# Mixture-of-experts weights in chunks of two channel tiles by 1024 features, experts overlapped, w2 dealt four rows to a partition

## The chip, the cores and the metric

The kernel runs on one NeuronCore of one Trainium2 chip. The metric is the device time of one execution in microseconds, as the median of three runs. The five engines that matter are PE (matrix multiply), ACT (activation), DVE (vector), POOL, and SP, which here only issues DMAs. Each engine works off its own list of instructions in a fixed order and waits on semaphores for the others.

## The reference

Two layers of a hybrid model for 256 tokens of width 1024. Each layer has a mixer; layer 0 has a dense feed-forward part and layer 1 a mixture of eight experts with top-2 routing. The change touches the experts only:

```
logits = (h @ router)
top_v, top_i = lax.top_k(logits, TOP_K)
gates = jnp.sum(one_hot(top_i, N_EXPERTS) * softmax(top_v)[..., None], axis=-2)
for e in range(N_EXPERTS):
    out = out + gates[..., e:e + 1] * ((silu(h @ w1[e]) * (h @ w3[e])) @ w2[e])
```

Here h is 256 x 1024, w1 and w3 are 1024 x 3584 per expert, and w2 is 3584 x 1024, all in fp32. One expert has 44 MB of weights, all eight 352 MB.

## The kernel before

Weights come as chunks of 1 MB (128 partitions x 2048 fp32) that `load` (L128) fetches on the SP queue into a tile called raw. `stream` (L150) lists all chunks in the order of use, `place` (L190) says which buffer each goes to, and `take` (L215) hands the next one to the multiplication. Chunk i of the experts goes to a ring of ten buffers: four of tag raw, one more in pool mp, and five from the pool act, whose twelve 8 KB buffers of tag big also hold everything else that is large (the gathered inputs X, the scaled outputs yy, the sum acc, the token-major inputs tm).

Every matrix product is done in three fp32r passes (`mm3`, L228). For that each chunk is split, by halves of 1024 columns, into a rounded part and a rest (`split_act`, L221): ACT writes whi (L222), then DVE writes wlo = raw - whi (L223). There are four whi and four wlo buffers, so half k can only be split once PE has finished with half k - 4. One half feeds two mm3, which is six matmuls of 512 columns. `take` puts the splits of chunk i + 1 ahead of the matmuls of chunk i.

`moe` (L1076) routes up to 128 tokens to each expert. `slots` and `gather` (L1125) build X for two experts at a time by 32 small matmuls gx that ACT and DVE copy out (L1138, L1140). For each expert, seven groups j of 512 features follow. A group takes four chunks of w1 and w3 (each 4 channel tiles x 512 features, 2 KB of a row at a time) into two PSUM tiles h; ACT applies Silu (L1221), DVE multiplies (L1222) into u; four PE transposes ut (L1229) turn u round, and ACT and DVE split the result into us (L222, L223). `down(j)` then multiplies us by two chunks of w2 (4 KB of a row at a time) into the two PSUM tiles y. It is called for group j - 1 while group j is under way, and for group 6 at the end of the expert. After that `gated` (L1158) scales y by the gate into yy (ACT L1160, DVE L1161), and `scatter` (L1146) sends yy back to the tokens by 16 small matmuls so, in four pieces that DVE adds to acc (L1156) during the next expert. The pieces are hung between the chunks by `step()`. The gather for the next pair of experts stands inside `down(5)` and `down(6)` of every second expert. ut, so, gx and two smaller tiles share two PSUM buffers of pool pm, tag m.

The framework's scheduler turns these calls into the fixed order of each engine, and gives out the buffers; a tile that finds no buffer free is put later in the order.

```
hi, lo for a half of a chunk:
        a = self.nc.scalar.activation(hi, x, AF.Copy)
        b = self.nc.vector.tensor_tensor(lo, x, hi.bitcast(F), op=OP.subtract)
```

Of the kernel before, what the change touches and what calls it, by code (L numbers as in the profile page):

```python
# [9 lines left out]
F = mybir.dt.float32  # L10
# [84 lines left out]
class Kernel:  # L95
# [54 lines left out]
    def stream(self):  # L150
# [26 lines left out]
        v1, v3, v2 = (a["moe_w%d" % i][0].rearrange("e (k p) f -> e p k f", p=P) for i in (1, 3, 2))  # L177
        for e in range(NE):
            last = e == NE - 1
            for j in range(7):  # L180
                out += [v[e, :, 4 * h:4 * h + 4, j * 512:(j + 1) * 512] for v in (v1, v3) for h in range(2)]
                if j and not last:
                    out += [v2[e, :, 2 * c:2 * c + 2, :] for c in (2 * j - 2, 2 * j - 1)]
            if last:
                out += [v2[e, :, 4 * c:4 * c + 4, n * 512:(n + 1) * 512] for n in range(2) for c in range(NET // 4)]
            else:
                out += [v2[e, :, 2 * c:2 * c + 2, :] for c in (12, 13)]
        return out

    def place(self, i):  # L190
# [4 lines left out]
        ring = ("raw",) * 4 + ("more",) + ("big",) * 5  # L195
        if i >= (NE - 1) * 42:
            return ring[i % 5]
        if i < 10 + self.early:
            return ring[min(i, 9)]
        return ring[(i - self.early) % 10]  # L200
# [651 lines left out]
    def mixer(self, l, h):  # L852
# [70 lines left out]
        def mid(c):  # L923
            if c == 2 and l == DEPTH - 1:
                self.ahead(self.moe0 + self.early + 10, 0)
# [149 lines left out]
    def moe(self, h, r):  # L1075
# [95 lines left out]
        side = []  # L1171
        for e in range(NE):
            us = []
            if e == 0:
                side = [r.gates, None]
            else:
                side = [None, None] + [lambda p=p, e=e: scatter(e - 1, p) for p in range(4)]
            if e % 2 == 0:
                side += [lambda e=e: slots_t(e)]
            if e == 1:  # L1180
                side.append(count)
            side = iter(side)

            def step():
# [3 lines left out]
            last = e == NE - 1  # L1188
            py = [self.py.tile([P, 512], F, name=self.nm("y"), tag="y") for _ in range(2)]
            yy = self.big(R, "yy")  # L1190
            Y[e] = yy[:, :D], yy[:, D:]
            g = gather(e + 1) if e % 2 and not last else iter(())

            def down(j):

                for c in range(2):
                    W = self.take()
                    for k in range(2):
                        f = 2 * c + k
                        for n in range(2):  # L1200
                            self.mm3(py[n], [t[:, f] for t in us[j]], [x[:, n * 512:(n + 1) * 512] for x in W[k]],
                                     j == 0 and f == 0, j == 6 and f == 3)
                    if j > 4:
                        next(g, None)
                        next(g, None)
            for j in range(7):
                hs = []
                for v in range(2):
                    ps = self.pg.tile([P, 512], F, name=self.nm("h"), tag="g")
                    for a in range(2):  # L1210
                        W = self.take()
                        self.behind = None
                        for k in range(4):
                            self.mm3(ps, [x[:, 4 * a + k] for x in X[e]], W[k],
                                     a == 0 and k == 0, a == 1 and k == 3)
                        for _ in g0:
                            pass
                        step()
                    hs.append(ps)
                u = self.sm([P, 512], name="u")  # L1220
                nc.scalar.activation(u, hs[0], AF.Silu)  # L1221
                nc.vector.tensor_tensor(u, u, hs[1], op=OP.mult)  # L1222
                if j and not last:
                    down(j - 1)
                if j == 1 and e % 2 and not last:
                    slots(e + 1)
                pt = self.pm.tile([P, 4, P], F, name=self.nm("ut"), tag="m")
                for i in range(4):
                    nc.tensor.transpose(pt[:, i], u[:, i * P:(i + 1) * P], self.c("ident"))  # L1229
                if not last:  # L1230
                    t = self.mp.tile([P, 2, 4, P], R, name=self.nm("us"), tag="us", bufs=2)
                elif j % 2 == 0:
                    t2 = self.big(R, "us").rearrange("p (j a b t) -> p j a b t", j=2, a=2, b=4)
                if last:
                    t = t2[:, j % 2]
                self.split_act(pt, t[:, 0], t[:, 1])
# [249 lines left out]
```

## Time and profile before

| | |
|---|---|
| median of three runs | 1959.42 us (1958.44 to 1960.45) |
| the profiled execution | 1957.16 us |
| its span, first to last instruction | 1955.4 us |
| mean granted TensorE clock | 0.984 |
| busy share of the span: PE, DVE, ACT | 95%, 81%, 65% |
| DMA | 540.10 MB, q1 77.9% of the 16 engines' time |
| chain that ended last | PE 88%, DVE 4%, ACT 3%, DMA 2% |

Busy time is the time in which an engine executes at least one instruction; matmuls overlap, so the pace of PE is read from the distance between their starts. The experts begin at about 933 us and end at about 1942 us of the span.

### The profile page before, as it was taken

What the parts mean: (1) busy time and instruction counts of PE and PEld (TensorE: products, weight loads), DVE (VectorE), ACT (ScalarE), POOL (GpSimd) and SP (SyncE); (2) the same over time, 40 slices, a digit from 0 to 9 for tenths busy, and PEclk for the clock granted to TensorE, in tenths of its full rate; (3) what the DMA queues carried; (4) which work ended last, traced back from release to release, by engine and by line L of the source; (5) the groups of instructions that cost most, each with busy time, mean ns of one, the idle gap of its engine ahead of it and who ended that gap; (6) DMA issues with size and microseconds to landing.
All of it is one profiled execution on the core that took longest, in us unless ns stands there. A gap on an engine that the chain in (4) does not pass through costs nothing.

```text
span 1955.4 us, 32539 instructions
## 1 busy us (share of the span) xinstructions
PE 1867.3 (95%) x13258; PEld 1647.6 (84%) x13258; DVE 1583.8 (81%) x1839; ACT 1273.9 (65%) x1514; POOL 8.1 (0%) x11
## 2 busy tenths in 40 slices
PE   6999999899989989998999999999999999999996
PEld 3988999799979989997887887878878877787885
DVE  4678866777766788676899998999989898899996
ACT  4664744444446737444787787877878777787884
POOL 0000000000000000000000000000000000000000
PEclk8999999999999999999999999999999999999998
DMA  9544676477754437877799998999989999897994
GB/s 316 194 148 148 226 263 214 141 242 262 298 173 138 142 122 245 266 262 280 251 362 328 362 380 304 367 360 359 375 295 378 374 333 355 329 349 268 339 355 146
DMA packets 293790, 540.10 MB, mean 276 GB/s; under 512 B 8704, under 2 KB 132224, under 8 KB 293632
## 3 DMA queue, kind: packets, MB, share of 16 engines
q1 hardware_dynamic: 293632, 537.93, 77.9%
q8 instruction: 106, 1.74, 0.4%
q14 instruction: 52, 0.43, 0.1%
HBM read 536.85 MB, written 1.05 MB: 275 GB/s over the span
## 4 chain that ended last, share of the span: by engine, by line
PE 88%; DVE 4%; ACT 3%; DMA 2%; issue 1%; SPq 0%; ACTq 0%; DVEq 0%
PE h L231 10%; PE h L230 10%; PE h L232 10%; PE ps L230 10%; PE ps L231 10%; PE ps L232 10%; PE y L232 5%; PE y L230 5%; PE y L231 5%; DMA raw<-in_w_ada 1%; DVE wlo L223 1%; PE ut L1229 1%; PE po L230 1%; PE po L231 1%; PE po L232 1%
## 5 line engine op out<-in xcount | busy, mean ns | idle before, releaser
L222 ACT ACTIVATE whi<-raw 128x1024 fp32r<-128x1024 f32 x910 | 959.1, 1060 | 494.5 <-PE ps L231 203.9
L223 DVE TENSOR_TENSOR wlo<-raw,whi 128x1024 fp32r<-128x1024 f32 x910 | 1095.7, 1222 | 185.2 <-ACT whi L222 154.0
L230 PE MATMUL ps<-hhi,whi 128*128 128x256 f32 x1216 | 347.2, 286 | 11.1 <-ACT hhi L422 10.9
L230 PE MATMUL h<-whi,X 128*128 128x512 f32 x896 | 353.7, 395 | 0.0
L231 PE MATMUL h<-wlo,X 128*128 128x512 f32 x896 | 350.5, 391 | 0.4 <-DVE wlo L223 0.4
L232 PE MATMUL h<-whi,X 128*128 128x512 f32 x896 | 350.1, 391 | 0.0
L231 PE MATMUL ps<-hlo,whi 128*128 128x256 f32 x1216 | 346.2, 285 | 0.1
L232 PE MATMUL ps<-hhi,wlo 128*128 128x256 f32 x1216 | 345.4, 284 | 0.1
L230 PEld LDWEIGHTS ps<-hhi,whi 128*128 128x128 f32 x1216 | 234.4, 193 | 14.2 <-ACT hhi L422 11.7
L231 PEld LDWEIGHTS ps<-hlo,whi 128*128 128x128 f32 x1216 | 234.5, 193 | 2.0 <-issue 1.0
L232 PEld LDWEIGHTS ps<-hhi,wlo 128*128 128x128 f32 x1216 | 234.3, 193 | 1.3 <-issue 0.8
L231 PEld LDWEIGHTS h<-wlo,X 128*128 128x128 f32 x896 | 168.7, 188 | 35.7 <-DVE wlo L223 3.0
L232 PEld LDWEIGHTS h<-whi,X 128*128 128x128 f32 x896 | 168.4, 188 | 35.3
L230 PEld LDWEIGHTS h<-whi,X 128*128 128x128 f32 x896 | 168.7, 188 | 32.9
L230 PE MATMUL y<-whi,us 128*128 128x512 f32 (+1 forms) x452 | 174.1, 389 | 4.3 <-ACT us L222 4.3
L231 PE MATMUL y<-wlo,us 128*128 128x512 f32 (+1 forms) x452 | 175.7, 389 | 0.4 <-DVE wlo L223 0.4
L232 PE MATMUL y<-whi,us 128*128 128x512 f32 (+1 forms) x452 | 174.7, 389 | 0.5 <-DVE us L223 0.5
L285 DVE SCALAR_TENSOR_TENSOR ada<-raw,ca,ada 128x1024 f32<-128x1024 f32 x70 | 89.7, 1282 | 44.0 <-DMA raw<-in_w_ada 43.6
L230 PEld LDWEIGHTS y<-whi,us 128*128 128x128 f32 x452 | 84.9, 188 | 22.4 <-ACT us L222 5.2
L232 PEld LDWEIGHTS y<-whi,us 128*128 128x128 f32 x452 | 84.6, 188 | 19.1 <-DVE us L223 1.8
L231 PEld LDWEIGHTS y<-wlo,us 128*128 128x128 f32 x452 | 84.9, 188 | 18.1 <-DVE wlo L223 1.3
L230 PE MATMUL ps<-ghi,whi 128*128 128x256 f32 x256 | 72.5, 283 | 0.0
(349 smaller groups left out, 2303.4 us busy)
## 6 DMA issues: line engine op xcount, KB each, us to landing
raw<-in_moe_w SPq DMA_DIRECT2D x336, 1024.0 KB, 6.4
raw<-in_w_in SPq DMA_DIRECT2D x64, 1024.0 KB, 6.9
raw<-in_w_ada SPq DMA_DIRECT2D x48, 1024.0 KB, 7.6
raw<-in_ffn_w SPq DMA_DIRECT2D x33, 1024.0 KB, 5.6
raw<-in_w_proj_a SPq DMA_DIRECT2D x8, 1024.0 KB, 7.2
raw<-in_w_proj_b SPq DMA_DIRECT2D x8, 1024.0 KB, 7.8
raw<-in_w_out SPq DMA_DIRECT2D x8, 1024.0 KB, 5.3
wbd<-in_wbd SPq DMA_DIRECT2D x8, 512.0 KB, 8.4
```

The source lines that it names most:

```text
L222: a = self.nc.scalar.activation(hi, x, AF.Copy)
L223: b = self.nc.vector.tensor_tensor(lo, x, hi.bitcast(F), op=OP.subtract)
L230: first = nc.tensor.matmul(ps, l[0], r[0], start=start, stop=False, **k)
L231: nc.tensor.matmul(ps, l[0], r[1], start=False, stop=False, **k)
L232: nc.tensor.matmul(ps, l[1], r[0], start=False, stop=stop, **k)
L285: o = nc.vector.scalar_tensor_tensor(acc, w, self.ca[:, k:k + 1], acc, op0=OP.mult, op1=OP.add)
L1229: nc.tensor.transpose(pt[:, i], u[:, i * P:(i + 1) * P], self.c("ident"))
```

## The change

Chunks of w1 and w3 become 2 channel tiles x 1024 features (4 KB of a row at a time); the last 512 of the 3584 features keep the old shape. The rows of w2 are dealt so that a partition holds four that follow one another; a chunk takes two of them (8 KB in one piece), and the columns of u are picked at a distance of four for the transposes, to match. An expert now has four groups j, three of 1024 features (two PSUM tiles and two of every step after them) and one of 512. The last `down` of an expert and its `gated` move behind the first group of the next expert. The small steps are hung at fixed places: scatter at chunks 11, 13, 15 and 17 of w1 and w3, the next gather at chunks 12, 14, ... 26 of every second expert. us moves from two buffers of its own in pool mp to the pool act (tag big), the ring of weight buffers becomes 4 raw + 2 in mp + 2 big, and loads are asked for ten chunks ahead in place of twelve.

```diff
-            raw = self.mp.tile([P, 2048], F, name=self.nm("raw"), tag="raw", bufs=1)
+            raw = self.mp.tile([P, 2048], F, name=self.nm("raw"), tag="raw", bufs=2)
...
+        v2 = a["moe_w2"][0].rearrange("e (b p i) c -> e b p i c", p=P, i=4)
         for e in range(NE):
             last = e == NE - 1
-            for j in range(7):
-                out += [v[e, :, 4 * h:4 * h + 4, j * 512:(j + 1) * 512] for v in (v1, v3) for h in range(2)]
-                if j and not last:
-                    out += [v2[e, :, 2 * c:2 * c + 2, :] for c in (2 * j - 2, 2 * j - 1)]
+            for j in range(4):
+                if j < 3:
+                    out += [v[e, :, 2 * h:2 * h + 2, j * 1024:(j + 1) * 1024] for v in (v1, v3) for h in range(4)]
+                else:
+                    out += [v[e, :, 4 * h:4 * h + 4, 3072:] for v in (v1, v3) for h in range(2)]
+                if j == 0 and e:
+                    out += [v2[e - 1, 6, :, 2 * c:2 * c + 2, :] for c in range(2)]
+                elif j and not last:
+                    out += [v2[e, b, :, 2 * c:2 * c + 2, :] for b in (2 * j - 2, 2 * j - 1) for c in range(2)]
...
-        ring = ("raw",) * 4 + ("more",) + ("big",) * 5
+        ring = ("raw",) * 4 + ("more",) * 2 + ("big",) * 2
...
-        self.ahead(i + 4 if i < self.moe0 else i + 10 + self.early, i + (3 if i + 1 in self.pairs else 2))
+        self.ahead(i + 4 if i < self.moe0 else i + 10, i + (3 if i + 1 in self.pairs else 2))
...
+            side = {}
+            if e == 0:
+                side[0] = r.gates
+            else:
+                for p in range(4):
+                    side[11 + 2 * p] = lambda p=p, e=e: scatter(e - 1, p)
+            if e % 2 == 0:
+                side[19] = lambda e=e: slots_t(e)
+            elif not last:
+                side[9] = lambda e=e: slots(e + 1)
+                g = gather(e + 1)
+                for i in range(8):
+                    side[12 + 2 * i] = lambda: next(g)
...
+            for j in range(4):
+                n = 2 if j < 3 else 1
+                u = []
                 for v in range(2):
+                    ps = [self.pg.tile([P, 512], F, name=self.nm("h"), tag="g") for _ in range(n)]
+                    up(e, ps, v, j, side)
+                    for i in range(n):
+                        if v == 0:
+                            u.append(self.sm([P, 512], name="u"))
+                            nc.scalar.activation(u[i], ps[i], AF.Silu)
+                        else:
+                            nc.vector.tensor_tensor(u[i], u[i], ps[i], op=OP.mult)
+                if j == 0 and e:
+                    down(*before, 3)
+                    halves(e - 1)
+                    for i in range(2):
+                        gated(e - 1, slice(i * 512, (i + 1) * 512), before[1][i])
...
                 if j and not last:
+                    down(us, py, j - 1)
+                t = self.big(R, "us").rearrange("p (a b t) -> p a b t", a=2, b=8)
+                for i in range(n):
+                    pt = self.pm.tile([P, 4, P], F, name=self.nm("ut"), tag="m")
+                    for k in range(4):
+                        nc.tensor.transpose(pt[:, k], u[i].rearrange("p (t k) -> p k t", k=4)[:, k], self.c("ident"))
+                    o = slice(4 * i, 4 * i + 4)
+                    self.split_act(pt, t[:, 0, o], t[:, 1, o])
```

The changed file's lines stand 5 further down for `split_act` and `mm3` (L227, L228, L235 to L237).

First place: DVE, before the change, in a middle group of the third expert. A product u is followed by five splits of weights and then by us of the same group; PE uses that us 48 h matmuls later.

```order
L1222 TENSOR_TENSOR u_12994<-u_12994,h_12949 128x512
L223 TENSOR_TENSOR wlo_13004<-raw_12735,whi_13003 128x1024
L223 TENSOR_TENSOR wlo_13022<-raw_12763,whi_13021 128x1024
L223 TENSOR_TENSOR wlo_13026<-raw_12763,whi_13025 128x1024
L223 TENSOR_TENSOR wlo_13053<-raw_12792,whi_13052 128x1024
L223 TENSOR_TENSOR wlo_13057<-raw_12792,whi_13056 128x1024
L223 TENSOR_TENSOR us_13046<-ut_13041,us_13046 128x512
```

DVE after the change, third expert, at the end of the short group (3072 to 3583). us_13411 belongs to the group before; its transposes came 48 h matmuls earlier.

```order
L228 TENSOR_TENSOR wlo_13503<-raw_13299,whi_13502 128x1024
L1238 TENSOR_TENSOR u_13471<-u_13471,h_13473 128x512
L228 TENSOR_TENSOR wlo_13522<-raw_13323,whi_13521 128x1024
L228 TENSOR_TENSOR wlo_13526<-raw_13323,whi_13525 128x1024
L228 TENSOR_TENSOR us_13411<-ut_13412,us_13411 128x512
L228 TENSOR_TENSOR us_13411<-ut_13419,us_13411 128x512
```

PE after the change at the same place: the last h matmuls of the short group, and right behind them the y matmuls that read us_13411.

```order
L235 MATMUL h_13473<-whi_13480,X_11826 128x512
L236 MATMUL h_13473<-wlo_13481,X_11826 128x512
L237 MATMUL h_13473<-whi_13480,X_11827 128x512
L235 MATMUL y_13013<-whi_13498,us_13411 128x512
L236 MATMUL y_13013<-wlo_13499,us_13411 128x512
L235 MATMUL y_13014<-whi_13498,us_13411 128x512
L237 MATMUL y_13013<-whi_13498,us_13411 128x512
```

The split of us has moved from long before its use to behind a product that itself waits for the last h matmul.

Second place: DVE after the change, fifth expert, end of the first group. The two products u of a group stand apart, with the two splits of one chunk between them.

```order
L228 TENSOR_TENSOR wlo_14860<-raw_14661,whi_14859 128x1024
L1238 TENSOR_TENSOR u_14803<-u_14803,h_14807 128x512
L228 TENSOR_TENSOR wlo_14878<-raw_14683,whi_14877 128x1024
L228 TENSOR_TENSOR wlo_14882<-raw_14683,whi_14881 128x1024
L1238 TENSOR_TENSOR u_14805<-u_14805,h_14808 128x512
```

PE after the change at that place: wlo_14878 is read by the matmuls behind the transposes.

```order
L237 MATMUL h_14808<-whi_14859,X_13995 128x512
L235 MATMUL y_14088<-whi_14877,us_14705 128x512
L235 MATMUL y_14089<-whi_14877,us_14705 128x512
L1252 MATMUL ut_14949<-cst,u_14803 128x128 x4
L236 MATMUL y_14088<-wlo_14878,us_14705 128x512
```

The first split of the down chunk now stands behind a product that waits for PE, where before the change a split of the next chunk had been done by then.

Third place: DVE after the change, third expert, end of its first group, where the scaling of the second expert's outputs has moved to.

```order
L228 TENSOR_TENSOR wlo_12914<-raw_12699,whi_12913 128x1024
L1166 SCALAR_TENSOR_TENSOR yy_12789<-y_11920,gs_10395,yy_12789 128x512
L1166 SCALAR_TENSOR_TENSOR yy_12789<-y_11921,gs_10395,yy_12789 128x512
L228 TENSOR_TENSOR us_12794<-ut_12795,us_12794 128x512
L228 TENSOR_TENSOR us_12794<-ut_12802,us_12794 128x512
L228 TENSOR_TENSOR wlo_12918<-raw_12699,whi_12917 128x1024
L1161 TENSOR_TENSOR acc_10396<-acc_10396,so_12899 128x512
```

Four steps that are no weight splits now stand in one row on DVE; before the change the scaling and us stood apart.

## Rows read from the trace of the kernel before

**Rows 1.** Busy time by stretch (us from the span's start), the experts and one undisturbed stretch

```profile
core 0: us, PE busy (x) PEld busy (x) DVE busy (x) ACT busy (x) POOL busy (x), PEclk, DMA share, GB/s
950.00:1930.00 980.00, 964.71 (x4440) 793.61 (x4439) 895.70 (x848) 766.37 (x806) 0.00 (x0) 1.00 0.94 343
1200.00:1300.00 100.00, 100.00 (x462) 82.86 (x461) 94.12 (x91) 79.89 (x83) 0.00 (x0) 1.00 0.98 359
```

**Rows 2.** DMA queue of SP in the experts' stretch: longest waits, issues

```profile
SPq L135 <- DVE wlo L223: 814.3, 264, 15.3
...
raw<-in_moe_w SPq DMA_DIRECT2D x321, 1024.0 KB, 6.4
```

**Rows 3.** PE in order of time, an undisturbed stretch: start, duration, instruction

```profile
1073.98 0.40 PE L232 MATMUL h<-whi,X 128*128 128x512 f32 x1
1074.21 0.60 PE L1229 MATMUL ut<-cst,u 128*128 128x128 f32 x4
1074.57 0.48 PE L230 MATMUL h<-whi,X 128*128 128x512 f32 x1
```

**Rows 4.** PE in order of time, end of the first expert; in brackets idle time, releaser

```profile
1052.45 0.60 PE L1229 MATMUL ut<-cst,u 128*128 128x128 f32 x4
1054.25 0.50 PE L230 MATMUL y<-whi,us 128*128 128x512 f32 x1 [1.19 <-ACT us L222]
...
1055.05 0.40 PE L231 MATMUL y<-wlo,us 128*128 128x512 f32 x1
1055.62 0.74 PE L232 MATMUL y<-whi,us 128*128 128x512 f32 x2 [0.17 <-DVE us L223]
```

**Rows 5.** The same, end of the second expert

```profile
1174.77 0.39 PE L232 MATMUL y<-whi,us 128*128 128x512 f32 x1
1176.79 0.74 PE L1135 MATMUL gx<-Pm,tm 128*128 128x256 f32 x4 [1.63 <-ACT X L1140]
1178.25 0.71 PE L1135 MATMUL gx<-Pm,tm 128*128 128x256 f32 x4 [0.73 <-DVE X L1138]
...
1179.75 0.74 PE L1135 MATMUL gx<-Pm,tm 128*128 128x256 f32 x4 [0.35 <-DVE X L1138]
```

**Rows 6.** The same, first scatter of the sixth expert

```profile
1581.90 0.39 PE L1152 MATMUL so<-PT,yy 128*128 128x256 f32 x1 [1.00 <-DVE yy L1161]
...
1583.31 0.66 PE L1229 MATMUL ut<-cst,u 128*128 128x128 f32 x4 [0.42 <-DVE acc L1156]
```

**Rows 7.** Waits from 950 to 1930 us: who for whom, us in total, times, longest

```profile
PE gx L1135 <- ACT X L1140: 4.9, 3, 1.6
PE y L230 <- ACT us L222: 4.3, 4, 1.2
...
PE gx L1135 <- DVE X L1138: 3.4, 6, 0.9
```

**Rows 8.** Instruction groups from 950 to 1930 us: count, busy us, mean ns, idle before

```profile
L223 DVE TENSOR_TENSOR wlo<-raw,whi 128x1024 fp32r<-128x1024 f32 x663 | 797.7, 1222 | 72.1 <-ACT whi L222 41.8
L222 ACT ACTIVATE whi<-raw 128x1024 fp32r<-128x1024 f32 x662 | 697.9, 1061 | 181.9 <-PE h L232 110.5 <-PE y L232 59.3 <-DVE wlo L223 10.8
...
L223 DVE TENSOR_TENSOR us<-ut,us 128x512 fp32r<-128x512 f32 x56 | 38.3, 685 | 6.0 <-ACT us L222 6.0
L1222 DVE TENSOR_TENSOR u<-u,h 128x512 f32<-128x512 f32 x56 | 38.1, 681 | 2.2 <-PE h L232 2.2
L222 ACT ACTIVATE us<-ut 128x512 fp32r<-128x512 f32 x56 | 32.7, 584 | 16.8 <-PE ut L1229 16.5
L1156 DVE TENSOR_TENSOR acc<-acc,so 128x512 f32<-128x512 f32 x26 | 17.5, 679 | 0.2 <-PE so L1152 0.2
...
L1161 DVE SCALAR_TENSOR_TENSOR yy<-y,gs,yy 128x512 fp32r<-128x512 f32 x15 | 10.7, 743 | 1.1 <-ACT yy L1160 1.1
```

**Rows 9.** ACT in order of time, end of the first expert

```profile
1051.29 1.07 ACT L222 ACTIVATE whi<-raw 128x1024 fp32r<-128x1024 f32 x1 [0.29 <-PE y L232]
1052.65 1.06 ACT L222 ACTIVATE whi<-raw 128x1024 fp32r<-128x1024 f32 x1 [0.30 <-PE y L232]
```

More of the change, by code (lines that the diff above doesn't have):

```diff
@@ L194, in place @@
             return "raw"
-        ring = ("raw",) * 4 + ("more",) + ("big",) * 5
+        ring = ("raw",) * 4 + ("more",) * 2 + ("big",) * 2
         if i >= (NE - 1) * 42:
[L197 to L200, printed above, removed]
+            return ring[i % 6]
+        if i < 12:
+            return ring[min(i, 7)]
+        return ring[(i - 4) % 8]
     def ahead(self, loads, splits):
@@ L924, in mid @@
             if c == 2 and l == DEPTH - 1:
-                self.ahead(self.moe0 + self.early + 10, 0)
+                self.ahead(self.moe0 + 12, 0)
             if c:
@@ L1170, in moe, with up @@
         self.behind = behind
[L1171 to L1184, printed above, removed]
+        def up(e, ps, v, j, side):
+            n = len(ps)
+            for a in range(2 * n):
+                W = self.take()
+                self.behind = None
+                for k in range(4 // n):
+                    t = 4 // n * a + k
+                    for i in range(n):
+                        self.mm3(ps[i], [x[:, t] for x in X[e]], [x[:, i * 512:(i + 1) * 512] for x in W[k]],
+                                 t == 0, t == KT - 1)
+                for _ in g0:
+                    pass
                 f = next(side, None)
@@ L1187, in step, with down @@
                     f()
-            last = e == NE - 1
-            py = [self.py.tile([P, 512], F, name=self.nm("y"), tag="y") for _ in range(2)]
+        def down(us, py, j):
+            for c in range(4 if j < 3 else 2):
+                W = self.take()
+                for k in range(2):
+                    f = 2 * c + k
+                    for n in range(2):
+                        self.mm3(py[n], [t[:, f] for t in us[j]], [x[:, n * 512:(n + 1) * 512] for x in W[k]],
+                                 j == 0 and f == 0, j == 3 and f == 3)
@@ L1190, in moe, with halves @@
+        def halves(e):
             yy = self.big(R, "yy")
             Y[e] = yy[:, :D], yy[:, D:]
[L1192 to L1205, printed above, removed]
@@ L1206, in moe @@
-            for j in range(7):
-                hs = []
-                for v in range(2):
[L1209 to L1222, printed above, removed]
-                if j and not last:
[L1224 to L1236, printed above, removed]
-                us.append((t[:, 0], t[:, 1]))
@@ L1238, in moe @@
-            if not last:
-                down(6)
-                for n in range(2):
-                    gated(e, slice(n * 512, (n + 1) * 512), py[n])
-            else:
+        before = None
+        for e in range(NE):
+            last = e == NE - 1
+            side = {}
[11 more added lines that the diff above has]
+                    side[12 + 2 * i] = lambda: next(g)
+            if e == 1:
+                side[21] = count
+            side = iter([side.get(i) for i in range(28)])
+            us = []
+            for j in range(4):
+                n = 2 if j < 3 else 1
+                u = []
+                for v in range(2):
+                    ps = [self.pg.tile([P, 512], F, name=self.nm("h"), tag="g") for _ in range(n)]
[11 more added lines that the diff above has]
+                        gated(e - 1, slice(i * 512, (i + 1) * 512), before[1][i])
+                if j == 1:
+                    py = [self.py.tile([P, 512], F, name=self.nm("y"), tag="y") for _ in range(2)]
+                if j and not last:
+                    down(us, py, j - 1)
+                t = self.big(R, "us").rearrange("p (a b t) -> p a b t", a=2, b=8)
+                for i in range(n):
+                    pt = self.pm.tile([P, 4, P], F, name=self.nm("ut"), tag="m")
[3 more added lines that the diff above has]
+                    self.split_act(pt, t[:, 0, o], t[:, 1, o])
+                us.append((t[:, 0], t[:, 1]))
+            before = us, py
+            if last:
+                halves(e)
@@ L1251, in moe @@
                                 f = 4 * c + k
-                                self.mm3(py[n][:, o:o + w], [t[:, k] for t in us[c]],
+                                self.mm3(py[n][:, o:o + w], [t[:, f % 8] for t in us[c // 2]],
                                          [x[:, o:o + w] for x in W[k]], f == 0, f == NET - 1, skip_group_check=True)
@@ L1340, in run @@
         self.fcount = 0
-        self.early = 2
         self.chunks = self.stream()
```

6 lines of the change are left out of this document (2 added, 4 removed).

## The prediction

> **What bounds the kernel now.** I read the busy times by stretch first. [...] Three resources are nearly full, so the question is which of them the others wait for. The DMA queue's own waits answer for the loads: SP waits 814.3 us, in 264 pieces, for DVE to free a weight buffer [rows 2], and no wait of ACT, DVE or PE in this stretch ends with a load. So a load that lands sooner only waits longer. The timeline of PE gives its pace: the start of one 512-column matmul lies 0.23 us behind the start of the one before, and a group of four transposes holds PE for 0.36 us [rows 3]. An expert has 504 such matmuls, 116 us of about 126 (eight experts from 933 to 1942 us), and the rest is transposes, gather, scatter and idle time. PE is the bound, and only its idle time and its count of instructions can be changed.
>
> That idle time stands at the changes of expert. At the end of the first expert the last transposes end at 1052.45 + 0.36 = 1052.81, but y starts at 1054.25, 1.44 late, because us has still to be split, and again 0.34 late at 1055.62 (1055.05 + 0.23 was possible) [rows 4]: 1.8 us. At the end of the second expert the gather waits for the two PSUM buffers that it shares: 1.79 late at 1176.79; then, with half of 0.23 for each 256-column matmul, 1.0 late at 1178.25 and 0.7 late at 1179.75 [rows 5]: 3.4 us. The waits say how often: y waited for us four times, 4.3 us in all with 1.2 the longest, and the gather for ACT three times, 4.9 us [rows 7]. The scatter of the sixth expert has 1.00 + 0.42 us more [rows 6].
>
> **What the change removes.** With the next expert's first group ahead of the last down, PE has work while us is split, and the gather is spread over the expert. That takes away 3 x 1.8 + 0.9 (the fourth y wait, the shortest), 3 x 3.4 and 1.4, together 17.9 us. The least that can be meant is the idle time alone, 4.3 + 4.9 + 3.4 + 1.4 = 14.0; the most, with rests too small for a row, I put at 20.
>
> **What it leaves as it is.** Bytes, chunks (336) and matmuls stay the same, and so do splits, transposes, gather and scatter. [...] SP's list has as many loads; the ring falls from ten buffers to eight, and at 3 us a chunk (1 MB at 343 GB/s [rows 1]) eight are 24 us ahead, against 6.4 us from issue to landing [rows 2]: 0 as long as that lead holds. POOL has no work here.
>
> **What it adds: waits behind DVE.** Work that fills the removed waits has to be ready, and this is decided by the order of DVE. A weight split costs ACT 1.06 and DVE 1.22 us per half; u costs DVE 0.68, a half of us 0.685 (ACT 0.58), a half of yy 0.74, a piece of acc 0.68 [rows 8]. A split can begin about when PE's last matmul on the half four before has ended (ACT idles until then, [rows 9]), and PE reaches the new half three halves later. One half is six matmuls, 1.36 us. So a wlo is done 2.3 us after the release and needed some 4.1 after it. DVE therefore runs 1.8 us ahead and no more, whatever its mean load.
>
> (a) First place in the section on the change. In the third expert us stands behind u and two wlo, u waits for the last h, and y follows at once. Counted from the end of the last h, DVE is through with the first us at 0.68 + 2 x 1.22 + 0.685 = 3.81. Unstalled, the matmul that reads it would start at 0.52 (the next start lies 0.16 before that end, since starts are 0.23 apart and a matmul takes 0.39, and three go ahead). Wait: 3.3 us. The seventh expert has the same order. In the second and sixth the gather stands behind the first y and needs both shared PSUM buffers, which the transposes hold until both halves of us are split: 0.68 + 2 x 1.22 + 2 x 0.685 = 4.49 against 0.53, so 4.0 us; in the second one split less stands behind u, but the split ahead of u ends only 0.92 after the last h, hence 0.92 + 0.68 + 1.22 + 1.37 = 4.19, 3.7 us. First, fourth and fifth expert have us ahead of the short group's end: 0. Sum 3.3 + 3.3 + 4.0 + 3.7 = 14.3 us. If only ACT's half of us counted, each would be about 2, so 8; with the sums of semaphore delays 17.
>
> (b) Second place. The first u can start 0.68 before the last h ends, so the wlo behind it ends at 1.22. PE can do two whi matmuls and four transposes before it needs it: -0.16 + 0.45 + 0.36 = 0.65. Wait: 0.6 us. This order occurs six times (third and seventh expert once, fifth twice, sixth and eighth once): 3.6 us, bounds 0 and 7.
>
> (c) Third place. yy, us and acc in one row are 2 x 0.74 + 2 x 0.685 + 0.68 = 3.5 us. The next wlo would be done at 2.3 + 3.5 + 1.2 = 7.0 after the release and is needed at 1.36 + 4.1 = 5.5, plus what PE does between: two matmuls and a scatter group, 0.45 + 0.47. It is 0.6 late, or on time where a gather group stands there too; two more u before the next down take what is left of the lead. I take 0.8 us for each of the seven changes of expert, 5.6 us, bounds 0 and 12.
>
> **Sum.** 14.3 + 3.6 + 5.6 = 23.5 us of new waits (8 to 36) against 17.9 removed (14 to 20): +5.6 us, bounds -12 and +22. The profiled execution took 1957.16 us (span 1955.4), 2.3 below the median of the runs, 1959.42; the sum made against it gives 1962.8, and against the median 1965.0. A measurement of this kernel can tell 0.2%, 3.9 us, from no change.
>
> **The rival that PE itself gets slower.** The weights of the new transposes are columns of u at a distance of four values, 16 bytes. Every weight load in the trace reads columns that lie side by side, so no row has a price for this. A load can hardly get cheaper; at one side it costs nothing more, at the other a load at half the rate makes the four transposes cost twice 0.36. Nothing covers that, because PE is the bound: 56 groups of four (224 instructions at four each) x 0.36 = 20 us, hence 1985. I give the free end the greater weight: no row speaks for either, and the columns differ in their distance alone. [...]
>
> **The rival that the gain stays.** If the new waits (a) are covered, because DVE gets to us while PE is still on the short group, only (b) and (c) are left at their lower halves, about 5 us: 1959.4 - 17.9 + 5 = 1946.5, faster. For it speaks that before the change matmuls waited for wlo in rows too small to matter, though DVE was at 91%. Against it: the order is fixed, and u cannot run before the last h has ended. It decides at about 12 us of new waits; below that the change is faster by more than 0.2%.
>
> **Smaller rivals.** The loads bound the experts after all with eight buffers, of which two are shared with X, us and yy: each chunk that is late by one load's 3 us costs that, and one per expert would be +24, 1989. For it speaks a DMA share of 0.94; against it, SP's 814 us of waiting. Or the experts don't run into one another at all, since us finds no buffer; then the old waits stay beside (b) and (c), 1959.4 + 9 = 1968.6, which lies in the forecast's range.
>
> **How the numbers follow.** The forecast has 0.50 and its own range 1950 to 1978; of it 0.05 is faster, 0.20 the same, 0.25 slower. The slower transposes, alone or with the rest, have 0.22 (1979 to 1999), the gain that stays 0.19 (1940 to 1955), late loads 0.05, and 0.04 I leave to the old waits staying. Faster by over 0.2%: 0.05 + 0.19 = 0.24. The same: 0.20. Slower: 0.25 + 0.22 + 0.05 + 0.04 = 0.56. Range 1944 to 1990: it cuts the lower end of the gain that stays and the upper end of the slower transposes, about one in ten on each side.
>
> **What would show it.** Right: PE without idle time at the changes of expert; in the second, third, sixth and seventh expert a gap of 3 to 4 us on PE behind the short group, ended by us; DVE, not a load, named for the small waits of y on wlo; transposes still at 0.36 for four. Wrong: four transposes at 0.5 us or more; waits of whi on a load; PE idle time in the experts below 10 us or above 40.

## The result, and the profile after

The changed kernel took 1969.76 us in the median of eight runs (1963.26 to 1972.97), the kernel before 1959.29 in the runs beside it: a ratio of 1.0051, 95% interval 1.0040 to 1.0062, so slower by 10.5 us. The profiled execution of the change is the longest of the eight (1972.97 us, span 1971.2). In it the first h of the experts starts 1.7 us later than before (938.29 against 936.63) and the last h 15.7 us later (1909.12 against 1893.38): the experts take 14.1 us longer.

The waits that the change was credited with removing [rows 4 to 7] are gone: no gather waits for ACT any more, and no y of an expert's last `down` for us. Waits of the changed kernel from 950 to 1930 us (who waits for whom, us in total, times, longest):

```profile
PEld y L235 <- ACT us L227: 8.2, 4, 2.1
...
PE y L235 <- ACT us L227: 6.5, 4, 1.6
...
PE gx L1140 <- DVE us L228: 3.4, 2, 2.0
PE y L237 <- DVE us L228: 2.9, 2, 1.5
...
PE y L236 <- DVE wlo L228: 2.5, 6, 0.7
```

PE now waits for us, in four places and in two steps each. As before, no engine waits there for a load, although the landing of one went from 6.4 to 7.4 us [rows 2]. PE in order of time, third expert, end of its short group:

```profile
1293.89 0.39 PE L237 MATMUL h<-whi,X 128*128 128x512 f32 x1
1295.91 0.50 PE L235 MATMUL y<-whi,us 128*128 128x512 f32 x1 [1.63 <-ACT us L227]
1296.25 0.40 PE L236 MATMUL y<-wlo,us 128*128 128x512 f32 x1
1296.49 0.40 PE L235 MATMUL y<-whi,us 128*128 128x512 f32 x1
1298.34 0.79 PE L237 MATMUL y<-whi,us 128*128 128x512 f32 x1 [1.46 <-DVE us L228]
1298.93 0.63 PE L236 MATMUL y<-wlo,us 128*128 128x512 f32 x1
1299.36 0.63 PE L237 MATMUL y<-whi,us 128*128 128x512 f32 x1
1299.79 0.63 PE L235 MATMUL y<-whi,us 128*128 128x512 f32 x1
```

And DVE at that place:

```profile
1294.73 0.68 DVE L1238 TENSOR_TENSOR u<-u,h 128x512 f32<-128x512 f32 x1
1295.33 2.35 DVE L228 TENSOR_TENSOR wlo<-raw,whi 128x1024 fp32r<-128x1024 f32 x2
1297.60 1.28 DVE L228 TENSOR_TENSOR us<-ut,us 128x512 fp32r<-128x512 f32 x2
```

u waits for the last h, two splits follow, then us: y starts 1.79 and 1.63 us behind PE's pace, 3.4 together. Behind it there is something that the prediction has no term for. From 1298.9 on the matmuls start 0.43 us behind one another, not 0.23 [rows 3]. The windows behind the four places (us; PE, PEld, DVE, ACT and POOL busy; granted clock; DMA share; GB/s) show the cause: the granted clock is 0.50 there, where the whole stretch of before has 1.00 [rows 1]:

```profile
950.00:1930.00 980.00, 963.49 (x4375) 793.95 (x4374) 869.78 (x834) 749.23 (x795) 0.00 (x0) 0.99 0.92 342
...
1171.50:1174.00 2.50, 2.50 (x7) 1.93 (x7) 0.28 (x1) 0.83 (x1) 0.00 (x0) 0.50 0.89 315
1298.50:1304.00 5.50, 5.50 (x13) 4.30 (x14) 1.94 (x3) 2.11 (x2) 0.00 (x0) 0.50 1.00 381
1677.50:1682.50 5.00, 5.00 (x16) 4.17 (x16) 1.03 (x2) 1.65 (x2) 0.00 (x0) 0.50 0.60 241
1807.00:1812.50 5.50, 5.50 (x14) 4.24 (x14) 1.94 (x3) 2.11 (x2) 0.00 (x0) 0.50 0.01 3
```

42 matmuls start 0.20 us late in this way, 8.4 us. In the sixth expert the clock has already fallen when the gather behind the wait starts, and its eight matmuls add 0.7 us (they start 0.21 us behind one another, elsewhere 0.12):

```profile
1674.34 0.49 PE L235 MATMUL y<-whi,us 128*128 128x512 f32 x1 [1.63 <-ACT us L227]
1676.86 2.04 PE L1140 MATMUL gx<-Pm,tm 128*128 128x256 f32 x8 [2.03 <-DVE us L228]
1678.70 0.63 PE L236 MATMUL y<-wlo,us 128*128 128x512 f32 x1
```

PE is 100% busy in these windows, so a table of busy time hides the loss; the clock column, the distance of the starts and the longer rows (0.63 us in place of 0.39) show it.

### The profile page after: what moved, and what is told of

It reads as the page before. It is cut to its first block, busy times and chain, and to the rows that moved or that the text cites. A ratio compares the mean times of both kernels' runs of the same rounds, so it can differ in the third digit from the quotient of the medians.

```text
span 1971.2 us, 32550 instructions
## 1 busy us (share of the span) xinstructions
PE 1883.0 (96%) x13258; PEld 1660.3 (84%) x13258; DVE 1573.3 (80%) x1839; ACT 1268.2 (64%) x1514; POOL 8.1 (0%) x11
## 2 busy tenths in 40 slices
DMA packets 232094, 540.10 MB, mean 274 GB/s; under 512 B 8704, under 2 KB 132224, under 8 KB 219392
## 4 chain that ended last, share of the span: by engine, by line
PE 88%; DVE 5%; ACT 3%; DMA 2%; issue 2%; SPq 0%; DVEq 0%; ACTq 0%
PE h L236 10%; PE ps L235 10%; PE h L235 10%; PE ps L236 10%; PE ps L237 10%; PE h L237 10%; PE y L236 5%; PE y L237 5%; PE y L235 5%; DVE wlo L228 2%; DMA raw<-in_w_ada 1%; PE ut L1252 1%; PE po L235 1%; PE po L237 1%; PE po L236 1%
## 5 line engine op out<-in xcount | busy, mean ns | idle before, releaser
L227 ACT ACTIVATE whi<-raw 128x1024 fp32r<-128x1024 f32 x910 | 951.4, 1061 | 505.8 <-PE ps L236 207.1
L228 DVE TENSOR_TENSOR wlo<-raw,whi 128x1024 fp32r<-128x1024 f32 x910 | 1083.5, 1222 | 211.4 <-ACT whi L227 186.6
L235 PE MATMUL ps<-hhi,whi 128*128 128x256 f32 x1216 | 347.2, 286 | 11.1 <-ACT hhi L427 10.9
L237 PE MATMUL h<-whi,X 128*128 128x512 f32 x896 | 349.6, 390 | 0.0
L237 PE MATMUL ps<-hhi,wlo 128*128 128x256 f32 x1216 | 345.4, 284 | 0.1
L235 PE MATMUL h<-whi,X 128*128 128x512 f32 x896 | 331.0, 392 | 0.0
L235 PEld LDWEIGHTS ps<-hhi,whi 128*128 128x128 f32 x1216 | 234.4, 193 | 14.2 <-ACT hhi L427 11.7
L237 PEld LDWEIGHTS ps<-hhi,wlo 128*128 128x128 f32 x1216 | 234.2, 193 | 1.4 <-issue 0.8
L237 PEld LDWEIGHTS h<-whi,X 128*128 128x128 f32 x896 | 168.4, 188 | 33.9
L235 PEld LDWEIGHTS h<-whi,X 128*128 128x128 f32 x896 | 168.5, 188 | 33.6
L236 PE MATMUL y<-wlo,us 128*128 128x512 f32 (+1 forms) x452 | 182.0, 403 | 2.5 <-DVE wlo L228 2.5
L237 PE MATMUL y<-whi,us 128*128 128x512 f32 (+1 forms) x452 | 180.0, 398 | 2.9 <-DVE us L228 2.9
L235 PE MATMUL y<-whi,us 128*128 128x512 f32 (+1 forms) x452 | 169.1, 396 | 6.5 <-ACT us L227 6.5
L235 PEld LDWEIGHTS y<-whi,us 128*128 128x128 f32 x452 | 86.9, 192 | 26.8 <-ACT us L227 8.2
L237 PEld LDWEIGHTS y<-whi,us 128*128 128x128 f32 x452 | 87.4, 193 | 21.2 <-DVE us L228 3.8
L235 PE MATMUL ps<-ghi,whi 128*128 128x256 f32 x256 | 72.5, 283 | 0.0
```

The costliest lines, as they stand in the source:

```text
L235: first = nc.tensor.matmul(ps, l[0], r[0], start=start, stop=False, **k)
L236: nc.tensor.matmul(ps, l[0], r[1], start=False, stop=False, **k)
L237: nc.tensor.matmul(ps, l[1], r[0], start=False, stop=stop, **k)
```

## The experiments

All ratios are to the kernel before, run on the same chip; the runs used several chips, so medians of different rows compare less closely than ratios do. The last column is the time from the first to the last h of the experts in each profile (before 956.8, the change 970.8 us).

| run | median us | ratio, 95% interval | first to last h |
|---|---|---|---|
| us_own | 1956.50 | 0.9986 (0.9977 to 0.9995) | 954.0 |
| cols_side_by_side | 1967.81 | 1.0049 (1.0036 to 1.0063) | 964.8 |
| cols_dealt_alone | 1961.80 | 1.0011 (1.0002 to 1.0020) | 959.5 |
| gap_filled | 1966.24 | 1.0041 (1.0027 to 1.0054) | 963.3 |
| join_alone | 1969.47 | 1.0050 (1.0037 to 1.0064) | 967.0 |
| us_two | 1958.08 | 0.9994 (0.9985 to 1.0003) | 956.3 |
| five_splits | 1960.36 | 1.0003 (0.9994 to 1.0012) | 954.1 |
| join_yy_own | 1959.84 | 1.0001 (0.9992 to 1.0010) | 957.4 |
| u_after_splits | 1945.12 | 0.9926 (0.9912 to 0.9940) | 943.1 |
| ask_six_ahead | 1959.61 | 1.0001 (0.9992 to 1.0010) | 956.3 |
| six_and_order | 1942.26 | 0.9916 (0.9903 to 0.9930) | 940.4 |
| six_u_order | 1944.94 | 0.9923 (0.9911 to 0.9936) | 942.3 |

**us_own.** Is it the buffer that makes us late?

```diff
-                t = self.big(R, "us").rearrange("p (a b t) -> p a b t", a=2, b=8)
+                if last:
+                    t = self.big(R, "us").rearrange("p (a b t) -> p a b t", a=2, b=8)
+                else:
+                    t = self.mp.tile([P, 2, 8, P], R, name=self.nm("us"), tag="us", bufs=1)
-        ring = ("raw",) * 4 + ("more",) * 2 + ("big",) * 2
+        ring = ("raw",) * 4 + ("more",) + ("big",) * 3
```

> The changed kernel with us back in a buffer of its own (one of 8 KB in pool mp, in place of the second raw there; the ring stays at eight: 4 raw, 1 in mp, 3 big; the last expert as changed). Theory A (us is late because it finds no free buffer in the pool that the loads share): the four gaps of 3.4 to 4.3 us behind the short groups are gone (14.6 us in the profile of the changed kernel), and with them the stretches at half the clock behind them (about 9.4 us), so 1969.8 - 24 = 1946 us, 1943 to 1951, which is faster than before the change. Rival B (DVE is behind whatever buffer us has): the gaps stay or move to another wait, 1963 to 1971. If only the gaps went and the clock still fell: about 1955.

The gaps and the stretches at half clock are gone, and us stands eight splits ahead of the short group's u on DVE. DVE of us_own, third expert, in order of time:

```profile
1281.16 1.29 DVE L228 TENSOR_TENSOR us<-ut,us 128x512 fp32r<-128x512 f32 x2 [1.18 <-ACT us L227]
1282.60 4.63 DVE L228 TENSOR_TENSOR wlo<-raw,whi 128x1024 fp32r<-128x1024 f32 x4
1288.31 4.63 DVE L228 TENSOR_TENSOR wlo<-raw,whi 128x1024 fp32r<-128x1024 f32 x4 [1.08 <-ACT whi L227]
1292.85 0.68 DVE L1238 TENSOR_TENSOR u<-u,h 128x512 f32<-128x512 f32 x1
```

Theory A has the gaps right and the time wrong: 13.3 us came back by the medians, not 24. Within the experts it is 16.8 us in the profiles, but they start 2.7 us later, which I have not traced; and the 24 was sized on the slowest run of the change. Waits of 0.57 us for wlo behind pairs of u rose from six to nine, and four others (0.6 three times, 1.17 once) are new.

**cols_side_by_side and cols_dealt_alone.** What do the transposes' columns cost? One takes them out of the change, the other puts them alone into the kernel before, each with the dealing of w2's rows that belongs to them.

```diff
-        v2 = a["moe_w2"][0].rearrange("e (b p i) c -> e b p i c", p=P, i=4)
+        v2 = a["moe_w2"][0].rearrange("e (b i p) c -> e b p i c", p=P, i=4)
-                        nc.tensor.transpose(pt[:, k], u[i].rearrange("p (t k) -> p k t", k=4)[:, k], self.c("ident"))
+                        nc.tensor.transpose(pt[:, k], u[i][:, k * P:(k + 1) * P], self.c("ident"))
```

> The changed kernel with w2's rows undealt: a chunk is two k tiles of one row each, as before the change, and the transposes read columns of u that lie side by side; all else as changed. If the strided weight loads cost what the trace of the changed kernel shows (208 ns in place of 140 ns for one, 0.87 in place of 0.72 us for a group of eight): 2.5 us less, 1965 to 1969, with gaps and clock falls as they were. By the rival of the prediction, in which they were to cost 20 us: about 1950. If the 8 KB packets carried something: slower than the changed kernel.

> The kernel before with this alone: w2's rows dealt four in a row to a partition (8 KB packets) and the columns of u picked at a distance of four for the transposes. The packets give nothing, since no engine waits for a load; 56 groups of four transposes cost 0.03 to 0.05 us more each: +2.5 us, 1960 to 1963. By the rival of the prediction: +20 us, 1979.

Weight loads of the transposes in the changed kernel (shortest, median and longest in ns, first and last start):

```profile
L1252 PEld LDWEIGHTS ut<-cst,u x224: 195/208/219, 963.9 to 1911.6; 128*128 128x128 f32 x112
```

and in cols_side_by_side:

```profile
L1252 PEld LDWEIGHTS ut<-cst,u x224: 137/140/146, 963.2 to 1905.2; 128*128 128x128 f32 x112
```

A load takes 68 ns more, but most of that lies beside the matmul ahead: summed from start to start, the transposes cost 1.6 us more with the dealt columns in the change and 2.2 us more in the kernel before. The times agree, but loosely: the difference of the first pair is inside its spread, and its profiles also differ in the half clock (42 slow matmuls against 25). In the second pair the ratio is 1.0011. The load became half as long again (208 ns against 140), not twice as long. From the kernel before to the change, packets fell from 293790 to 232094, and no run shows time that came of it.

**gap_filled.** Is the half clock a consequence of PE standing still?

```diff
+                if j == 3 and e in (1, 2, 5, 6):
+                    pf = self.pg.tile([P, 512], F, name=self.nm("fl"), tag="g")
+                    for _ in range(14):
+                        m = nc.tensor.matmul(pf, X[e][0][:, 0], xf[e // 2 * 2][:, :512], start=True, stop=True)
+                        self.after(m, self.mm)
```

> The changed kernel with 14 matmuls of 512 columns more (3.2 us at 0.227 us each) on PE behind the last h of the short group of the second, third, sixth and seventh expert, where PE waits for us; their result is read by nothing. Theory C (the clock falls because PE stands still there, and the fall costs about 9 us on top of the gaps): the time of the gaps stays as it is but is spent at work, no stretch at half the clock behind them, 1960 to 1964 us, that is 6 to 9 us faster with 56 matmuls more. Rival D (the falls have another cause, the strided transposes or the load on all engines): 1968 to 1971, falls as before.

PE of gap_filled, third expert (compare the rows of the change above):

```profile
1293.32 0.39 PE L237 MATMUL h<-whi,X 128*128 128x512 f32 x1
1293.55 3.33 PE L1251 MATMUL fl<-X 128*128 128x512 f32 x14
1296.73 0.39 PE L235 MATMUL y<-whi,us 128*128 128x512 f32 x1
1296.95 0.39 PE L236 MATMUL y<-wlo,us 128*128 128x512 f32 x1
```

With 56 matmuls more no matmul between 950 and 1930 us starts at half the clock, and the granted clock is 1.00 from 1293 to 1304 us and around the other three places, though the dealt columns and the load on the other engines are still there. So theory C holds on the cause of the falls. Their price is less certain. The profiles give 9.1 us in the change (the matmuls of y and the gather) and 5.0 in cols_side_by_side (25 matmuls; of its four gaps, which are as long as those of the change, three are followed by a fall). By the medians gap_filled is 3.5 us faster than the change; taken as ratios to the kernel before it is 2.0, and the two intervals overlap (gap_filled also has 1.1 us more of waits for wlo). The runs of gap_filled lie within 1.8 us, those of the change within 9.7. The mean granted clock of the change's runs goes with this spread, from 0.984 in the fastest (1963.26 us) to 0.978 in the slowest (1972.97); so gaps of this kind need not cost the same in every run.

**join_alone and join_yy_own.** The joining of experts alone, in the kernel before: the last `down` and `gated` move behind the next expert's first group, scatter and gather to the places that they have in the change. The second run also has yy in a buffer of its own.

```diff
+                if j == 0 and e:
+                    down(*before, 6)
+                    halves(e - 1)
+                    for i in range(2):
+                        gated(e - 1, slice(i * 512, (i + 1) * 512), before[1][i])
...
-            yy = self.big(R, "yy")
+            yy = self.mp.tile([P, 2048], R, name=self.nm("yy"), tag="yy", bufs=1) if e < NE - 1 else self.big(R, "yy")
```

> The kernel before with this alone: an expert's last down and its scaling stand behind the next expert's first group, the scatter is hung at steps 11, 13, 15, 17 and the next gather at steps 12 to 26. Groups stay at 512 features with one u each, us keeps its two buffers, the ring its ten, w2's rows their order. The prediction's credit (17.9 us of idle time at the changes of expert) is then had without its debit: us stands five splits behind u, never behind the next u, and no two u follow each other. With 2 to 4 us for the few DVE steps that now stand in a row: 1958.8 - 17.9 + 3 = 1944 us, 1940 to 1948. Rival (the idle time is not recovered by joining, but moves into waits for DVE wherever the steps are put): 1953 to 1962.

> join_alone with yy in a buffer of its own (8 KB in pool mp, in place of the raw buffer there; the ring falls to nine: 4 raw and 5 big). In join_alone the scaling yy of the second to fifth expert stands some 12 weight splits behind the last matmul that it reads, and PE waits for it, for the next y that needs its PSUM buffers and for u behind it: the waits of 0.7 to 2.3 us that come in threes (1206, 1332, 1462, 1590 us), 18 us together, and 6 us of half clock behind them. Theory E (a tile that is taken from the pool which the loads share, us in the change, yy here, is put late in the order of ACT and DVE, and that is what costs, not the joining): all of these go, 1969.5 - 24 = 1945 us, 1941 to 1949. Rival F (joining puts more on DVE at that place than it can hold, whatever buffer yy has): waits for wlo take their place, 1955 to 1970.

PE of join_alone in the third expert:

```profile
1204.55 0.39 PE L232 MATMUL h<-whi,X 128*128 128x512 f32 x1
1206.59 0.66 PE L1237 MATMUL ut<-cst,u 128*128 128x128 f32 x4 [1.65 <-DVE u L1225]
1208.51 0.38 PE L1151 MATMUL so<-PT,yy 128*128 128x256 f32 x1 [1.27 <-ACT yy L1160]
1209.32 0.50 PE L230 MATMUL y<-whi,us 128*128 128x512 f32 x1 [0.42 <-DVE yy L1161]
```

yy came from the pool of the loads before, too, but at the start of the expert; here it is asked for behind the joined `down`. It stands nine splits behind the last y that it reads, late as us is in the change, and the half clock follows (32 matmuls, 6.3 us). In the change yy stands 2 to 12 splits behind that y in six of the seven experts, and PE does not wait for it there. With its own buffer yy stands next to the y that it reads, and waits and half clock are gone. But the time only comes down to that of before, because h now waits for wlo in 18 places of 0.51 to 0.74 us. Waits of join_yy_own from 950 to 1930 us:

```profile
ACT us L222 <- PE ut L1237: 74.0, 32, 2.6
...
PEld h L231 <- DVE wlo L223: 28.1, 56, 1.0
...
PE h L231 <- DVE wlo L223: 7.3, 18, 0.6
```

ACT stands 74 us at us until PE has made the transposes, with the next weight splits queued behind; that these waits make wlo late is argued, no run takes them away. Theory E is right on the gaps, rival F on the time.

**us_two and five_splits.** Two attempts on the waits for wlo that remain in us_own: a second buffer for us, and a fifth pair for the split weights (with the columns side by side).

```diff
-                    t = self.mp.tile([P, 2, 8, P], R, name=self.nm("us"), tag="us", bufs=1)
+                    t = self.mp.tile([P, 2, 8, P], R, name=self.nm("us"), tag="us", bufs=2)
...
-            hi = self.wp.tile([P, 1024], R, name=self.nm("whi"), tag="whi", bufs=self.nhi)
+            pool, n = (self.mp, 1) if five else (self.wp, self.nhi)
+            hi = pool.tile([P, 1024], R, name=self.nm("whi"), tag="whi", bufs=n)
```

> The changed kernel with us in two buffers of its own of 8 KB (both raw buffers of mp go, the ring is 4 raw and 4 big). With one such buffer (us_own) ACT stands 32 us in 18 waits at us until PE has left the last us, and DVE gets to the weights later: nine waits of 0.57 us behind a pair of u in place of six, three of 0.6 and one of 1.2 us. If that queue behind the waiting us was the loss, those waits go back to six: us_own's 1956.5 less 3 to 5, 1951 to 1954. If the pair of u on DVE makes them whatever us does: 1955 to 1957.

> us_own (one buffer of its own for us) with a fifth pair of buffers for the split weights (in pool mp, in place of the last raw buffer there; ring of 4 raw and 4 big) and with the transposes' columns side by side. DVE may then run one half, 1.36 us, further ahead of PE, which is more than any of the waits left (0.57 to 1.17 us): 1956.5 - 2 (columns) - 9 (the waits named) = 1945, 1942 to 1948. If the waits do not depend on how far DVE may run ahead (DVE saturated over a longer stretch): 1953 to 1955, the columns alone.

Both missed. Nine waits behind pairs of u stay in either, at 0.57 and 0.65 us: a buffer more did not help work that stands behind a waiting instruction. In five_splits the experts also start 3.2 us later than in us_own; ACT waits once 4.7 us for a load of theirs there, and why only in this run was not tried.

**u_after_splits, ask_six_ahead, six_and_order, six_u_order.** The order itself. The first is us_own with side-by-side columns and this edit, in which `self.lo` is the split of weights asked for last:

```diff
-                            nc.vector.tensor_tensor(u[i], u[i], ps[i], op=OP.mult)
+                            m = nc.vector.tensor_tensor(u[i], u[i], ps[i], op=OP.mult)
+                            if n == 2:
+                                self.after(m, self.lo)
```

The second is the changed kernel with one number changed, and us in the pool as in the change:

```diff
-        self.ahead(i + 4 if i < self.moe0 else i + 10, i + (3 if i + 1 in self.pairs else 2))
+        self.ahead(i + 4 if i < self.moe0 else i + 6, i + (3 if i + 1 in self.pairs else 2))
```

six_u_order has both edits, six_and_order the side-by-side columns as well.

> us_own with the columns side by side and with the two products u of a group of 1024 put behind the splits of the next down's first chunk on DVE (an order between instructions, no wait). The fifth pair of buffers left the nine waits of y for wlo behind a pair of u as they were (0.57, then 0.65 us), so it is not how far DVE may run ahead but the first u, which waits for the last h with a split queued behind it (the prediction's (b)). Then these nine waits go: 1956.5 - 2 (columns) - 5 = 1949.5 us, 1947 to 1953. If another split is then late in their place: 1954 to 1956.

> The changed kernel with one number changed: loads are asked for six chunks ahead, not ten; us stays in the pool of the loads. Theory G (us, asked for in that pool, comes behind all loads asked for before it; the lead of ten chunks is what puts it behind the short group's u): with six, us of the group before stands ahead of that u on DVE in the second, third, sixth and seventh expert, so the gaps of 3.4 to 4.3 us are gone (14.6 us in the profile) and the half clock behind them (4 to 9 us): 1969.8 - 19 to 24 = 1946 to 1951; with waits that return elsewhere, as in us_own, up to 1957. Rival (six chunks of 3 us are too short a lead for a load of 7.4 us): waits of ACT for loads in the experts, 1960 or more.

> ask_six_ahead with the columns side by side and the two products u of a group of 1024 behind the splits of the next down's first chunk. Against u_after_splits (1945.1) it spares the waits of ACT at us for PE, since us has several buffers again (34 us in 18 waits there). If those waits still make weights late: 1940 to 1944. If nothing hangs on them: 1944 to 1947. If the short lead makes loads late: above 1950.

> six_and_order with w2's rows dealt again and the transposes' columns at a distance of four, so that it differs from ask_six_ahead in the order of u alone and from six_and_order in the columns alone. The order takes away the 17 waits of 0.57 us behind pairs of u (9.3 us in ask_six_ahead's profile) and what they push back behind them: 1959.6 - 9 to 15, and the columns cost about 2 us as in the two runs on them: 1944 to 1946. If the price of the columns was partly hidden behind waits until now: 1946 to 1949. If the columns cost nothing here: 1942.

The order of u gave more than its waits: u_after_splits is 11.4 us below us_own, where 7 were expected (2 for the columns). The lead of six removed the four gaps and the half clock, without any wait for a load, so the lead of ten is what put us behind u; but its time is that of before, since now a pair of u holds up wlo 17 times (0.49 to 0.57 us, 9.3 us). This is the scheduler's order, too: u, two splits, u stands at 7 of the 24 pairs of u in the change, at 11 in us_own and at 17 here; at nearly all others the two u follow each other. DVE of ask_six_ahead, third expert:

```profile
1268.98 0.69 DVE L1238 TENSOR_TENSOR u<-u,h 128x512 f32<-128x512 f32 x1 [2.16 <-PE h L237]
1269.59 2.35 DVE L228 TENSOR_TENSOR wlo<-raw,whi 128x1024 fp32r<-128x1024 f32 x2
1271.86 0.68 DVE L1238 TENSOR_TENSOR u<-u,h 128x512 f32<-128x512 f32 x1
```

DVE idles 2.16 us in front of u while a split that could run stands behind it. In six_u_order the same place reads:

```profile
1257.49 9.16 DVE L228 TENSOR_TENSOR wlo<-raw,whi 128x1024 fp32r<-128x1024 f32 x8
1266.58 1.28 DVE L1238 TENSOR_TENSOR u<-u,h 128x512 f32<-128x512 f32 x2
1267.79 2.35 DVE L228 TENSOR_TENSOR wlo<-raw,whi 128x1024 fp32r<-128x1024 f32 x2
```

None of the 17 is left, and the time falls by 14.7 us, more than the waits themselves; where the rest comes from was not traced. six_and_order, 1942.26 us, is the best version: 0.84% (0.70 to 0.97) faster than before, 27.5 us faster than the change. From 950 to 1930 us PE is busy 975.96 us in it. Between six_u_order and six_and_order the columns make 2.7 us, but the intervals overlap.

## Why the prediction was right or wrong

Forecast 1965.0 us, measured 1969.8: the sign, the size within 5 us and the main cause were right. But two terms were wrong, (c) too large and the clock left out, and they partly cancel, so that the number came this near is in part luck.

- **What goes, 17.9 us.** Right: none of these waits is left in the change. That they were credited in full was right too, as the runs without the debits show (956.8 before, 940.4 in six_and_order, whose own waits for wlo are about 2 us).
- **(a), us behind the short group's u, 14.3 us.** Right in place, count and size. Late against PE's pace: 3.4 us in the third and seventh expert (forecast 3.3), 3.4 in the second (3.7), 4.1 in the sixth (4.0), together 14.3; the 4.3 and 14.6 in the expectations above are slightly too large. The semaphore delays in its upper bound of 17 were an estimate without a row; in the third expert, above, PE follows the first half of us by 0.06 us (1297.60 + 0.68 to 1298.34). The prediction took the order as given. The runs show where it comes from: us, and yy in join_alone, come late when they are asked for in the pool of the loads; a buffer of its own, or loads asked for six ahead, put us early. That requests are served in line is the reading that fits all of these, and no run looks at the line itself.
- **(b), a split behind the first u, 3.6 us.** Right, nearly in count: seven waits, 0.57 us six times and 0.49 once, 3.9 together, since the eighth expert has two where one was forecast. What the prediction could not see is that their number is a matter of the order: the edits that take (a) away also lay splits between more pairs of u, and then there are 9 or 17 such waits.
- **(c), a row of DVE steps at the expert change, 5.6 us.** Mis-sized: two waits, 0.50 and 0.16 us. The row in the third expert is yy and us only, 1224.29 to 1226.81, with acc a split later, as the third place in the section on the change has it too; the next split ends at 1228.03, and PE comes to it at 1228.30, behind two groups of so. The step that failed is the need time, which allowed for one such group, and the row was taken 1 us too long by counting acc. DVE and PE there:

```profile
1224.29 1.41 DVE L1166 SCALAR_TENSOR_TENSOR yy<-y,gs,yy 128x512 fp32r<-128x512 f32 x2 [0.33 <-ACT yy L1165]
1225.61 1.28 DVE L228 TENSOR_TENSOR us<-ut,us 128x512 fp32r<-128x512 f32 x2
1226.81 1.22 DVE L228 TENSOR_TENSOR wlo<-raw,whi 128x1024 fp32r<-128x1024 f32 x1
...
1228.30 0.39 PE L236 MATMUL h<-wlo,X 128*128 128x512 f32 x1
```

- **A missing term: the clock.** Idle time was counted once, for its length. Four gaps cost another 9.1 us in the profiled execution, the slowest of the eight, and some 2 to 5 by the medians. The one run at a mean clock of 0.984 took 1963.26 us, close to the forecast, which has no such term.
- **Columns at 16 bytes.** Taken as 0, with 20 us as a rival; they cost 1.6 to 2.2 us. The rival priced the whole group by its load; the loads lie mostly beside the matmuls ahead.
- **Packets, ring of eight: 0.** Right; in the change, with eight buffers, and in ask_six_ahead, with a lead of six, no engine waits for a load in the experts (in five_splits, also with eight, ACT waits twice, 2.0 us together). No run shows that wider packets shorten a load: from issue to landing one took 7.4 us in the change against 6.4 before.

In the profile: -17.9 + 14.3 + 3.9 + 0.7 + 9.1 + 1.6 to 2.2 = 11.7 to 12.3 of 14.1 us. The other 2 us I have not traced. The rival "the gain stays" (1946.5 us) is what the idea is worth once the order is mended: 1942 to 1945.

## What to carry to other kernels

Where an engine's list is fixed, ask of every instruction that waits what stands behind it that could have run: moving two products behind two splits was worth 9 to 15 us here, while a second buffer for us or a fifth pair for the split weights gave nothing. A tile that is asked for in a pool shared with prefetched loads may come late because of the depth of the prefetch, so give it a buffer of its own or shorten the lead. After such an edit read the whole order again: here it also moved other instructions, and a new kind of wait took the place of the one removed.

## What was not expected of the hardware

Two waits of PE, 1.63 and 1.46 us with three matmuls between, were followed by 5.5 us at half the clock, during which every matmul of 512 columns took 0.43 us from start to start. The waits at the expert change of before (1.63, 0.73 and 0.35 us with gather groups between, [rows 5]) were not: the clock stays at 1.00 there. But the waits do not decide it alone. In cols_side_by_side the seventh expert has the waits of the third, and the clock stays at 1.00, with the last two matmuls 0.23 us from start to start:

```profile
1800.67 0.50 PE L235 MATMUL y<-whi,us 128*128 128x512 f32 x1 [1.63 <-ACT us L227]
...
1803.08 0.50 PE L237 MATMUL y<-whi,us 128*128 128x512 f32 x1 [1.44 <-DVE us L228]
1803.41 0.39 PE L236 MATMUL y<-wlo,us 128*128 128x512 f32 x1
1803.64 0.40 PE L237 MATMUL y<-whi,us 128*128 128x512 f32 x1
```

In cols_dealt_alone, on the other hand, one of three changes of expert with the waits of before (1.63, 0.73 and 0.16 us, at 1428 us) was followed by some 3 us at the lower clock. What makes the difference no run here shows. With the gaps filled with work that nobody reads, the falls were gone, at the price of 56 matmuls and still no slower than with the gaps empty (1966.24 us against 1969.76). And weights at a distance of 16 bytes load in 208 ns against 140, of which PE's pace shows little (1.6 us for the 224 loads of the change, 2.2 in the kernel before).
